# Shared rotary key in a two-layer encoder: a split-weight section of its own, or a column-tiled fp32 group on raw tokens

## The chip, the cores and the metric

One core of a Trainium2 chip. The metric is the device time of one execution in microseconds (us); a profile shows one execution, and the times are the median and the range of three.

## What is computed

Two encoder layers over 1024 tokens of width 1024, float32 throughout, then a final RMSNorm. Each layer normalises the tokens and projects them once; latent attention with 8 heads and a gated depthwise convolution of 31 taps share that projection. A gated feed-forward part follows. The part of the reference that matters here:

```
h = _rmsnorm(x, g_mix[l])
p = h @ w_in[l]
c_q = _rmsnorm(p[..., :o1], g_q[l])
...
c_kv = _rmsnorm(p[..., o1:o2], g_kv[l])
...
k_rope = _apply_rope(p[..., o2:o3], cos, sin)
...
a, gt = jnp.split(p[..., o3:], 2, axis=-1)
u = a * jax.nn.sigmoid(gt)
u = _dwconv(u, w_dw_conv[l], b_dw_conv[l])
```

`k_rope`, the shared rotary key, has 32 columns, common to all heads. `_apply_rope` needs each half of the key times cos, and the other half times sin.

## The kernel before

Features lie on partitions and tokens along the free axis: a tile is 128 features by 1024 tokens, in two halves of 512. A float32 operand is split into a rounded part (h) and a remainder (l), both fp32r, and a product takes three fp32r matmuls (high by high, high by low, low by high). The tokens are split once per layer into `hl` (xs_kh, xs_kl) with g_mix multiplied in; the row norm `rx` is applied when a product leaves PSUM.

`project` runs a layer's projections as sections on TensorE (PE). The first three, g0, a0 and g1 (gates and values of the convolution), are in `first_sections` (layer 0) and `next_sections` (layer 1). Then follow a1, g2, a2, g3, a3, kv0, kv1, kr, q0, q1, q2, k0 to k3, u0, u1 and n0 to n3, in the order of the list `seq`. Three wide PSUM slots go round: a section waits until the one three places ahead of it has been evicted by VectorE (DVE) or ScalarE (ACT). `u0` so takes the slot of `k1`, whose last reader is DVE's `kl_1` (L673).

The order on DVE is set by a planner in `project`. Each evicting routine is a generator that yields the DVE time it used and the time until its next step is due; `work(until)` runs the steps that are due, in between the convolution's near taps (`conv_step`, L1719, 1.28 us in the plan), until the DVE clock reaches the PE clock. `SECTION` holds the planned PE times of the short sections, all others count 10.9. The far taps (L1725) are multiplied on ACT and added up by accumulating transfers that GpSimd (POOL) issues. What is left of the near taps when the sections are through is placed by `work(1e9)`, ahead of attention.

The shared key is the section kr (L733 to L739). Its weight tile holds the 32 columns, rotated copy included, as 64 high and 64 low columns side by side, so that 32 fp32r matmuls of 128x512 do it. POOL casts the high part and adds up the low one, ACT negates (L180). `key_rope` (L628 to L650) then copies the lower half out of PSUM, adds it to the upper one, multiplies by rx, cos and sin, adds the two halves and splits the result for attention.

The roots of a row norm are computed by `root` and `roots`: PE turns the sums of squares (`rq0t`, L248), DVE reduces them (L259) and takes nine small steps (L263 to L271).

Of the kernel before, what the change touches and what calls it, by code (L numbers as in the profile page):

```python
# [13 lines left out]
ALU = mybir.AluOpType  # L14
# [40 lines left out]
LEAD, TURN = 33.0, 22.0  # L55
SECTION = {"kr": 7.3, "k": 2.72, "u": 4.08, "n": 4.08, "v": 2.72}
TAP = 1.28
# [59 lines left out]
class Encoder:  # L117
# [32 lines left out]
    def weight_source(self, l, name):  # L150
        a = self.a
        kind, j = name[:-1], name[-1]
        if name == "kr":
            return a["w_kr"][l]
        if name == "v":
            return a["w_v"][l]
        if name == "k":
            return a["w_k"][l].rearrange("j p c -> p j c")
        if kind == "u":
            return a["w_uq"][l, 2 * int(j):2 * int(j) + 2].rearrange("j p c -> p j c")  # L160
        return a["w_in"][l, int(j) + {"a": 0, "g": 4, "kv": 8, "q": 10}[kind]]

    def cast(self, l, name, tag="ws"):
        src = self.weight_source(l, name)
        if name != "kr":
            return self.cast_tile(src, f"w{name}{l}", tag)
        w = self.tmp(tag, f"w{name}{l}", F32R, (128, 8, 128))
        hi, lo = w[:, :, 0:64], w[:, :, 64:128]
        src = src.rearrange("p (k m) -> p k m", k=8)
        self.nc.gpsimd.dma_start(out=hi, in_=src)  # L170
        return w, hi, lo, src

# [212 lines left out]
    def first_sections(self, l, supply):  # L385
# [19 lines left out]
        def load_x(k, c=every):  # L405
            nc.sync.dma_start(out=x[k][:, c], in_=self.xd[0][k][:, c])
# [25 lines left out]
        for k in range(2, 8):  # L432
            load_x(k)
        self.ident = self.const("ident", [128, 128], self.a["ident"])
        nc.vector.tensor_copy(out=self.ones_r, in_=self.ones)
# [38 lines left out]
        for k, i in order:  # L474
# [3 lines left out]
            if (k, i) == (6, 2):  # L478
                rx = self.blk(f"rx{l}")
                for s, r in zip(HALVES, self.spread(dg, f"rx{l}", HALVES, self.bank)):  # L480
                    nc.scalar.copy(out=rx[:, s], in_=r)
        supply(-8.0)
        return hl, rx, dict(zip(names, ps))

    def next_sections(self, l, nxt, supply):
# [8 lines left out]
        for c in range(2):  # L494
            for i in range(3):
                if (c, i) == (0, 0):
                    self.upper_first(ps[i], self.tiled(w[i]), nxt["hl"], HALVES[c])
                for k in range(8 if c or i else 0):
                    self.partial(ps[i], self.tiled(w[i]), nxt["hl"], k, (c,))
                if c == 1 and i == 0:  # L500
                    self.norm_root(l, nxt, 1, self.bank)
                if c == 1 and i == 1:
                    self.norm_spread(l, nxt, 1, self.bank)
        return nxt["hl"], nxt["r"], dict(zip(names, ps))

    def upper_first(self, ps, weights, moving, c, n=8):
# [11 lines left out]
    def project(self, l, carry):  # L518
# [101 lines left out]
        def queries_norm():  # L620
# [4 lines left out]
            for t in (st["cos"], st["sin"]):  # L625
                nc.vector.tensor_tensor(out=t, in0=t, in1=r, op=ALU.mult)
                yield 1.25, 0.0

        def key_rope():
            p, cos, sin = ps["kr"], st["cos"], st["sin"]  # L630
            t = self.blk(f"krt{l}")
            nc.scalar.copy(out=t[0:64, :], in_=p[64:128, :])
            yield 0.0, 1.5
            nc.vector.tensor_tensor(out=t[0:64, :], in0=p[0:64, :], in1=t[0:64, :], op=ALU.add)
            nc.vector.tensor_tensor(out=t[0:64, :], in0=t[0:64, :], in1=rx[0:64, :], op=ALU.mult)
            nc.vector.tensor_tensor(out=t[0:32, :], in0=t[0:32, :], in1=cos[0:32, :], op=ALU.mult)
            nc.vector.scalar_tensor_tensor(out=t[32:64, :], in0=t[32:64, :], scalar=self.freq[32:64, 1:2],
                                           in1=sin[32:64, :], op0=ALU.mult, op1=ALU.mult)
            t2 = self.blk(f"krt2{l}")
            nc.scalar.copy(out=t2[0:32, :], in_=t[32:64, :])  # L640
            yield 5.0, 1.5
            nc.vector.tensor_tensor(out=t[0:32, :], in0=t[0:32, :], in1=t2[0:32, :], op=ALU.add)
# [90 lines left out]

        def shared_key():
            for k in range(8):
                for s in range(2):
                    for c in HALVES:
                        nc.tensor.matmul(ps["kr"][:, c], w["kr"][:, k, :], hl[k][s][:, c],
                                         start=(k == 0 and s == 0), stop=(k == 7 and s == 1))  # L739

        def inputs(name):
# [18 lines left out]
        def rooted(out):  # L760
# [5 lines left out]
            return st.pop(out)  # L766

        seq = []
        add = lambda name, weight, emit, evict, after=None: seq.append((name, weight, emit, evict, after))
# [9 lines left out]
        for j in range(2):  # L779
            add(f"kv{j}", f"kv{j}", inputs(f"kv{j}"), lambda j=j: latent(f"kv{j}", ckv, "kss", j))  # L780
        add("kr", "kr", shared_key, key_rope)
        add("q0", "q0", inputs("q0"), lambda: query_latent(0), lambda: root("kss", "kroot", KVL, "rkv"))
# [30 lines left out]
        launch(glu(0), -2)  # L813
        launch(gate(1), -1)
        for n, (name, weight, emit, evict, after) in enumerate(seq):
            supply(clock["pe"])
# [379 lines left out]
    def down_steps(self, l, steps, put):  # L1196
# [155 lines left out]
        def resume():  # L1352
            if not last:
                nxt["w"] = [self.cast(l + 1, n) for n in ("g0", "a0", "g1")]

        put(end - 1, 6, resume)
# [458 lines left out]
def _layout(inputs):  # L1815
# [14 lines left out]
    out["w_in"] = tiles(w_in, np.r_[o3:o3 + 2 * CONV, o1:o2, 0:o1])  # L1830
    kr = w_in[:, :, np.r_[o2:o3, o2 + HALF:o3, o2:o2 + HALF]].reshape(DEPTH, 8, 128, 64)
    out["w_kr"] = c(kr.transpose(0, 2, 1, 3)).reshape(DEPTH, 128, 512)
    hd = NOPE + ROPE
# [44 lines left out]
```

## Time and profile before

| | us |
|---|---|
| median of three runs | 2251.2 |
| range of the three | 2250.36 to 2254.52 |
| the profiled execution, its own time | 2251.68 |
| its span, first to last instruction | 2249.9 |
| PE busy in it | 2225.7 (99%) |
| DVE busy | 1687.8 (75%) |
| ACT busy | 1235.2 (55%) |
| POOL busy | 693.4 (31%) |

The profile shows one execution. Its page groups instructions by source line and tile; the timeline gives every instruction with its start and duration in us, and in brackets how long its engine was idle before it and which instruction released it. PE's rows print matmuls, PEld's their weight loads.

### The profile page before, as it was taken

How to read it: one execution, taken by the hardware profiler on the slowest of the kernel's cores; microseconds unless marked ns; L12 is line 12 of the kernel's file. 1: busy time of each engine (PE TensorE's matmuls, PEld its weight loads, DVE VectorE, ACT ScalarE, POOL GpSimd, SP SyncE). 2: the span in 40 equal slices, each digit the busy share in tenths (PEclk: the TensorE clock that was granted, in tenths of full speed). 3: DMA queues.
4: the chain of work that ended last, by engine and by line, in shares of the span. 5: the costliest groups of instructions: out<-in, count | busy, mean ns of one | idle time of the engine just before them, and what ended most of it. 6: DMA issues, size and time to landing. Idle time of an engine off the chain costs nothing. (4 is left out here: it accounts for less than half of the span.)

```text
span 2249.9 us, 34444 instructions
## 1 busy us (share of the span) xinstructions
PE 2225.7 (99%) x12746; PEld 1790.3 (80%) x12746; DVE 1687.8 (75%) x2241; ACT 1235.2 (55%) x1885; POOL 693.4 (31%) x781
## 2 busy tenths in 40 slices
PE   9999999999999999999999999999999999999998
PEld 7887666888888888888888876668888888888887
DVE  6998898669777776776559778876787777768765
ACT  5444777447655555544523457774475555555444
POOL 1221586332333332002412226652323333320032
PEclk9999999999999999999999999999999999999999
DMA  6889998765999998935968999986669999988356
GB/s 186 162 171 279 193 216 184 206 174 125 227 269 304 276 300 206 331 106 144 207 133 167 201 265 198 196 197 177 159 155 232 291 291 278 292 211 300 102 127 168
DMA packets 201160, 472.85 MB, mean 210 GB/s; under 512 B 28352, under 2 KB 35616, under 8 KB 200992
## 3 DMA queue, kind: packets, MB, share of 16 engines
q0 software_dynamic: 102704, 220.91, 48.9%
q1 hardware_dynamic: 98000, 249.35, 33.6%
q8 instruction: 100, 1.64, 0.3%
q14 instruction: 68, 0.56, 0.1%
q10 hardware_dynamic: 288, 0.39, 0.0%
HBM read 306.14 MB, written 80.40 MB: 172 GB/s over the span
## 5 line engine op out<-in xcount | busy, mean ns | idle before, releaser
L1078 PE MATMUL p<-b,w 128*128 128x512 f32 x3552 | 808.1, 389 | 0.2
L1078 PEld LDWEIGHTS p<-b,w 128*128 128x128 f32 x3552 | 665.9, 188 | 141.8 <-DVE w L1456 1.7
L1266 PE MATMUL pd<-ab,wd 128*128 128x512 f32 (+1 forms) x1920 | 422.3, 381 | 0.0
L1266 PEld LDWEIGHTS pd<-ab,wd 128*128 128x128 f32 x1920 | 350.8, 188 | 69.4 <-DVE ab L1456 0.4
L181 POOL DMA_DIRECT2D w<-wu x96 | 84.4, 879 | 358.9 <-ACT w L180 323.8
L1520 DVE TENSOR_REDUCE mx<-s 128x1 f32<-128x1024 f32 x128 | 156.2, 1220 | 37.1 <-PE s L1518 28.7
L1528 ACT ACTIVATE p<-s,mx 128x1024 f32<-128x1024 f32 x128 | 142.8, 1116 | 59.2 <-DVE mx L1520 57.3
L1468 DVE SCALAR_TENSOR_TENSOR o<-zg,par,o 128x1023 f32<-128x1023 f32 x88 | 112.8, 1283 | 76.7 <-ACT o L1462 75.3
L181 POOL DMA_DIRECT2D w<-in_w_up x116 | 100.5, 867 | 200.2 <-ACT w L180 179.0
L1719 DVE SCALAR_TENSOR_TENSOR conv<-gate,par,conv 128x1009 f32<-128x1009 f32 (+7 forms) x112 | 142.3, 1274 | 3.6 <-ACT conv L577 1.0
L180 ACT ACTIVATE w<-w 128x512 fp32r<-128x512 f32 x212 | 133.5, 630 | 3.0
L1454 ACT CAST ab<-ac 128x512 fp32r<-128x512 f32 x130 | 80.1, 617 | 97.7 <-DVE ac L1201 95.5
L1027 DVE TENSOR_TENSOR zg<-p,zg 128x512 f32<-128x512 f32 x88 | 60.5, 690 | 97.0 <-PE p L1078 90.3
L1567 PE MATMUL o<-pt,v 128*64 128x256 f32 x1024 | 126.8, 386 | 2.8 <-DVE yt L1581 1.6
L852 POOL DMA_DIRECT2D wd<-in_w_down x44 | 32.4, 738 | 308.5 <-PE pd L1266 165.2
L1468 DVE SCALAR_TENSOR_TENSOR v<-zv,par,v 128x1023 f32<-128x1023 f32 x88 | 112.4, 1279 | 10.5 <-ACT v L1462 10.4
L1454 ACT CAST w<-wu 128x512 fp32r<-128x512 f32 x84 | 51.8, 619 | 123.9 <-DVE wu L1027 121.3
L1541 PEld LDWEIGHTS t<-ident,p 64*128 64x128 f32 x2048 | 77.9, 138 | 41.1 <-issue 27.1
L1045 ACT CAST w<-wu 128x512 fp32r<-128x512 f32 x96 | 58.9, 614 | 92.9 <-DVE wu L1027 89.2
L1567 PEld LDWEIGHTS o<-pt,v 128*64 128x64 f32 x1024 | 67.9, 136 | 52.5 <-issue 18.5
L1544 DVE COPY pt<-t 128x512 f32<-128x512 f32 x128 | 87.5, 683 | 28.0 <-PE t L1541 26.8
L1738 POOL DMA_DIRECT2D conv<-late x75 | 68.3, 924 | 123.6 <-DVE late L1732 54.3
(2142 smaller groups left out, 4396.0 us busy)
## 6 DMA issues: line engine op xcount, KB each, us to landing
w<-in_w_up POOLq DMA_DIRECT2D x232, 256.0 KB, 7.4
wu<-in_w_up SPq DMA_DIRECT2D x88, 512.0 KB, 5.6
w<-wu POOLq DMA_DIRECT2D x96, 256.0 KB, 5.8
sd<-in_w_down SPq DMA_DIRECT2D x44, 512.0 KB, 9.8
ws<-sd SPq DMA_DIRECT2D x44, 512.0 KB, 6.9
wd<-in_w_down POOLq DMA_DIRECT2D x88, 256.0 KB, 5.3
act<-v SPq DMA_DIRECT2D x36, 512.0 KB, 5.7
ac<-act SPq DMA_DIRECT2D x72, 256.0 KB, 6.1
```

Of the source, the lines that this page charges most:

```text
L180: self.nc.scalar.activation(out=lo, in_=hi.bitcast(F32), func=AF.Copy, scale=-1.0)
L181: self.nc.gpsimd.dma_start(out=lo, in_=src, accum_op=ALU.add)
L1078: nc.tensor.matmul(ps, w[p][:, k * 128:(k + 1) * 128], b[:, q], start=(i in (1, 5, 2) and k == 0 and t == 0), stop=(k == 3 and t == 2), sk ...
L1266: nc.tensor.matmul(ps[t, m][:, cs], w[i, j][p][:, m * 128:(m + 1) * 128], b[:, q, cs], start=(i in (1, 5, 2) and j == 0 and s == 0), stop= ...
L1454: nc.scalar.copy(out=t[:, 0], in_=src)
L1468: self.nc.vector.scalar_tensor_tensor(out=o[:, a:b], in0=z[:, at + a:at + b], scalar=self.par[l][:, tap:tap + 1], in1=o[:, a:b], op0=ALU.m ...
L1520: nc.vector.tensor_reduce(out=mx, in_=ps, op=ALU.max, axis=AX.X, negate=True)
L1528: nc.scalar.activation(out=p, in_=ps, func=AF.Exp, bias=mx, accum_out=st["sums"][:, qt:qt + 1])
L1541: nc.tensor.transpose(t[:, i, qi, :], st["p"][2 * qp + qi][r, ks], self.ident[r, r])
L1544: nc.vector.tensor_copy(out=pt[:, :, :, 1, :], in_=tp[1])
L1567: nc.tensor.matmul(po[ROW_TILES[i % 2], cs], v[k // 2][:, k % 2, h * 64:h * 64 + 64], pt[:, i, :], start=k < 2, stop=k > 5)
L1719: self.nc.vector.scalar_tensor_tensor(out=y[:, lo:hi], in0=u[:, lo + s:hi + s], scalar=self.tap(l, j, t), in1=y[:, lo:hi], op0=ALU.mult, o ...
```

## The change

The section kr goes, and its entry in `SECTION` with it. `shared_weight` loads the 32 plain columns as one float32 tile of 128x256 (eight blocks of 32 columns) by SyncE (SP). `shared_key` multiplies it by g_mix on DVE, and then runs 16 plain fp32 matmuls of 32x512 on the raw tokens x, four groups of four: the four tiles of 32 weight columns take two blocks of rows and two token halves. It stands behind the first three sections in layer 0, and behind the first half of g1 in layer 1. Four ACT copies bring the tiles to `krt` and `krt2`; `key_sum`, launched with the first gates, adds them, multiplies by rx and makes the copy with its halves swapped by two SP transfers of 16x1024. `key_rope` runs behind kv1 and starts at the products with cos and sin. The branches for kr in `weight_source` and `cast` go.

```diff
@@ -53,7 +53,7 @@
 LEAD, TURN = 33.0, 22.0
-SECTION = {"kr": 7.3, "k": 2.72, "u": 4.08, "n": 4.08, "v": 2.72}
+SECTION = {"k": 2.72, "u": 4.08, "n": 4.08, "v": 2.72}
 TAP = 1.28
@@ -431,6 +423,7 @@
             load_x(k)
+        wk = self.shared_weight(l)
         self.ident = self.const("ident", [128, 128], self.a["ident"])
@@ -480,6 +473,7 @@
         supply(-8.0)
+        self.shared_key(l, wk, x)
         return hl, rx, dict(zip(names, ps))
@@ -497,11 +491,32 @@
                     self.partial(ps[i], self.tiled(w[i]), nxt["hl"], k, (c,))
+                if c == 0 and i == 2:
+                    self.shared_key(l, nxt["wk"], nxt["x"])
                 if c == 1 and i == 0:
...
         return nxt["hl"], nxt["r"], dict(zip(names, ps))
+
+    def shared_weight(self, l):
+        w = self.blk(f"wkr{l}", F32, (128, 8, ROPE))
+        self.nc.sync.dma_start(out=w, in_=self.a["w_kr"][l].rearrange("p (k m) -> p k m", k=8))
+        return w
+
+    def shared_key(self, l, w, x):
+        nc = self.nc
+        g = self.par[l][:, P_GMIX:P_GMIX + 8].unsqueeze(2).broadcast_to([128, 8, ROPE])
+        nc.vector.tensor_tensor(out=w, in0=w, in1=g, op=ALU.mult)
+        ps = self.bank(f"pkr{l}")
+        for i in range(4):
+            for q in range(4):
+                k = 2 * i + q % 2
+                nc.tensor.matmul(ps[q * ROPE:(q + 1) * ROPE, :], w[:, k, :], x[k][:, HALVES[q // 2]], start=i == 0, stop=i == 3,
+                                 tile_position=(0, q * ROPE))
+        self.kr = self.blk(f"krt{l}"), self.blk(f"krt2{l}")
+        for q in range(4):
+            nc.scalar.copy(out=self.kr[q % 2][0:ROPE, HALVES[q // 2]], in_=ps[q * ROPE:(q + 1) * ROPE, :])
 
@@ -626,19 +641,22 @@
 
+        def key_sum():
+            t, t2 = self.kr
+            nc.vector.tensor_tensor(out=t[0:32, :], in0=t[0:32, :], in1=t2[0:32, :], op=ALU.add)
+            nc.vector.tensor_tensor(out=t[0:32, :], in0=t[0:32, :], in1=rx[0:32, :], op=ALU.mult)
+            for i in range(2):
+                nc.sync.dma_start(out=t[32 + i * HALF:48 + i * HALF, :], in_=t[HALF - i * HALF:ROPE - i * HALF, :])
+            yield 2.5, 0.0
+
         def key_rope():
-            p, cos, sin = ps["kr"], st["cos"], st["sin"]
-            t = self.blk(f"krt{l}")
-            nc.scalar.copy(out=t[0:64, :], in_=p[64:128, :])
-            yield 0.0, 1.5
-            nc.vector.tensor_tensor(out=t[0:64, :], in0=p[0:64, :], in1=t[0:64, :], op=ALU.add)
-            nc.vector.tensor_tensor(out=t[0:64, :], in0=t[0:64, :], in1=rx[0:64, :], op=ALU.mult)
+            t, cos, sin = self.kr[0], st["cos"], st["sin"]
             nc.vector.tensor_tensor(out=t[0:32, :], in0=t[0:32, :], in1=cos[0:32, :], op=ALU.mult)
...
                                            in1=sin[32:64, :], op0=ALU.mult, op1=ALU.mult)
-            t2 = self.blk(f"krt2{l}")
+            t2 = self.blk(f"krt3{l}")
             nc.scalar.copy(out=t2[0:32, :], in_=t[32:64, :])
-            yield 5.0, 1.5
+            yield 2.5, 1.5
             nc.vector.tensor_tensor(out=t[0:32, :], in0=t[0:32, :], in1=t2[0:32, :], op=ALU.add)
@@ -731,13 +749,6 @@
 
-        def shared_key():
-            for k in range(8):
-                for s in range(2):
-                    for c in HALVES:
-                        nc.tensor.matmul(ps["kr"][:, c], w["kr"][:, k, :], hl[k][s][:, c],
-                                         start=(k == 0 and s == 0), stop=(k == 7 and s == 1))
-
         def inputs(name):
@@ -765,6 +776,11 @@
 
+        def shared_latent(j):
+            yield from latent(f"kv{j}", ckv, "kss", j)
+            if j:
+                yield from key_rope()
+
         seq = []
@@ -777,8 +793,7 @@
         for j in range(2):
-            add(f"kv{j}", f"kv{j}", inputs(f"kv{j}"), lambda j=j: latent(f"kv{j}", ckv, "kss", j))
-        add("kr", "kr", shared_key, key_rope)
+            add(f"kv{j}", f"kv{j}", inputs(f"kv{j}"), lambda j=j: shared_latent(j))
         add("q0", "q0", inputs("q0"), lambda: query_latent(0), lambda: root("kss", "kroot", KVL, "rkv"))
@@ -812,6 +827,7 @@
         launch(gate(1), -1)
+        launch(key_sum(), 0)
         for n, (name, weight, emit, evict, after) in enumerate(seq):
@@ -1352,6 +1368,7 @@
                 nxt["w"] = [self.cast(l + 1, n) for n in ("g0", "a0", "g1")]
+                nxt["wk"] = self.shared_weight(l + 1)
 
@@ -1828,8 +1845,8 @@
     out["w_in"] = tiles(w_in, np.r_[o3:o3 + 2 * CONV, o1:o2, 0:o1])
-    kr = w_in[:, :, np.r_[o2:o3, o2 + HALF:o3, o2:o2 + HALF]].reshape(DEPTH, 8, 128, 64)
-    out["w_kr"] = c(kr.transpose(0, 2, 1, 3)).reshape(DEPTH, 128, 512)
+    kr = w_in[:, :, o2:o3].reshape(DEPTH, 8, 128, ROPE)
+    out["w_kr"] = c(kr.transpose(0, 2, 1, 3)).reshape(DEPTH, 128, 8 * ROPE)
     hd = NOPE + ROPE
```

The plan moves instructions beyond the diff. Three places on DVE, word for word as the programs have them; `conv_3` is the convolution's fourth block of channels, `128x1018` the length of a near tap. In layer 0 between q1's squares (`qss_1`) and the remainder of the second normalised latent (`kvs_1l`), before:

```order
L607 TENSOR_TENSOR qss_1127<-qss_1127,qss_1_1232 128x1024
L660 SCALAR_TENSOR_TENSOR kvs_0l<-ckv_918,par_63,kvs_0h 128x1024
L616 TENSOR_TENSOR ckv_968<-ckv_968,rkv_1153 128x1024
L1719 SCALAR_TENSOR_TENSOR conv_3_845<-gate_3_777,par_63,conv_3_845 128x1018
L660 SCALAR_TENSOR_TENSOR kvs_1l<-ckv_968,par_63,kvs_1h 128x1024
```

and in the changed program:

```order
L622 TENSOR_TENSOR qss_1110<-qss_1110,qss_1_1215 128x1024
L678 SCALAR_TENSOR_TENSOR kvs_0l<-ckv_950,par_63,kvs_0h 128x1024
L631 TENSOR_TENSOR ckv_1022<-ckv_1022,rkv_1136 128x1024
L1736 SCALAR_TENSOR_TENSOR conv_3_878<-gate_3_809,par_63,conv_3_878 128x1012
L1736 SCALAR_TENSOR_TENSOR conv_3_878<-gate_3_809,par_63,conv_3_878 128x1013
L678 SCALAR_TENSOR_TENSOR kvs_1l<-ckv_1022,par_63,kvs_1h 128x1024
```

One tap stood ahead of `kvs_1l`, now two, and they are earlier taps. In layer 0 around the remainder of the second key section (`kl_1`) and the root for the queries (`rq0t`), before:

```order
L660 SCALAR_TENSOR_TENSOR cqs_2l<-cq_1269,par_63,cqs_2h 128x1024
L1719 SCALAR_TENSOR_TENSOR conv_3_845<-gate_3_777,par_63,conv_3_845 128x1020
L673 TENSOR_TENSOR kl_1_1328<-pk_1273,kh_1_1327 128x1024
L259 TENSOR_REDUCE rq0t<-rq0t 128x4 x2
L263 TENSOR_SCALAR rq0v<-rq0t 128x8
L264 TENSOR_SCALAR rq0y<-rq0v 128x8
```

and in the changed program:

```order
L251 TENSOR_REDUCE rq0t<-rq0t 128x4 x2
L255 TENSOR_SCALAR rq0v<-rq0t 128x8
L256 TENSOR_SCALAR rq0y<-rq0v 128x8
L257 TENSOR_TENSOR rq0t<-rq0y 128x8
L258 TENSOR_TENSOR rq0t<-rq0t,rq0v 128x8
L259 SCALAR_TENSOR_TENSOR rq0t<-rq0t 128x8
L260 SCALAR_TENSOR_TENSOR rq0y<-rq0t,rq0y 128x8
L261 TENSOR_TENSOR rq0t<-rq0y 128x8
L262 SCALAR_TENSOR_TENSOR rq0t<-rq0t,rq0v 128x8
L263 SCALAR_TENSOR_TENSOR rq0y<-rq0t,rq0y 128x8
L691 TENSOR_TENSOR kl_1_1312<-pk_1257,kh_1_1311 128x1024
L691 TENSOR_TENSOR kl_2_1338<-pk_1298,kh_2_1337 128x1024
```

`kl_1` stood ahead of the reduction; now it stands behind the reduction and its nine small steps. In layer 1 it is the same, and there three taps stand between q1's squares and `kl_1` that stood earlier before. In layer 0 at the end of the projections, where DVE turns to attention (`v_0` a copy of the values, `mx_0_0` the first row maximum), before:

```order
L721 SCALAR_TENSOR_TENSOR qn_1_1551<-qn_1_1551,qns_1_1553 128x1024
L721 SCALAR_TENSOR_TENSOR qn_2_1574<-qn_2_1574,qns_2_1576 128x1024
L721 SCALAR_TENSOR_TENSOR qn_3_1578<-qn_3_1578,qns_3_1580 128x1024
L1506 COPY v_0_1609<-pv_1_1611 128x512
L1520 TENSOR_REDUCE mx_0_0_1640<-s_0_0_1629 128x1
```

and in the changed program:

```order
L739 SCALAR_TENSOR_TENSOR qn_3_1562<-qn_3_1562,qns_3_1564 128x1024
L1736 SCALAR_TENSOR_TENSOR conv_3_878<-gate_3_809,par_63,conv_3_878 128x1018
L1736 SCALAR_TENSOR_TENSOR conv_3_878<-gate_3_809,par_63,conv_3_878 128x1019
L1736 SCALAR_TENSOR_TENSOR conv_3_878<-gate_3_809,par_63,conv_3_878 128x1020
L1736 SCALAR_TENSOR_TENSOR conv_3_878<-gate_3_809,par_63,conv_3_878 128x1021
L1736 SCALAR_TENSOR_TENSOR conv_3_878<-gate_3_809,par_63,conv_3_878 128x1022
L1523 COPY v_0_1598<-pv_1_1600 128x512
L1537 TENSOR_REDUCE mx_0_0_1629<-s_0_0_1618 128x1
```

Five taps now stand between the last query remainder and the first copy. In layer 1 no tap stands there, before or now. On SP the two transfers of the key's copy stand ahead of the load of the positions in layer 0, and ahead of the loads of cos and sin in layer 1.

## Rows read from the trace of the kernel before

**Rows 1.** Page: busy time by engine; shares of the chain of waits.

```profile
PE 2225.7 (99%) x12746; PEld 1790.3 (80%) x12746; DVE 1687.8 (75%) x2241; ACT 1235.2 (55%) x1885; POOL 693.4 (31%) x781
...
PE 39%; DVE 2%; issue 1%; DMA 1%; ACT 0%; POOL 0%; DVEq 0%; POOLq 0%; SPq 0%; ACTq 0%
```

**Rows 2.** Timeline of PE, layer 0's shared key: start us, duration us, operation.

```profile
118.95 0.62 PE L738 MATMUL pkr<-xs_0h,wkr 128*128 128x512 f32 x2
...
126.21 0.62 PE L217 MATMUL pq<-xs_0h,wq00h 128*128 128x512 f32 x2
```

**Rows 3.** Windows, shared key alone: length; busy PE, PEld, DVE, ACT; clock; DMA.

```profile
0.00:2249.00 2249.00, 14.83 (x64) 12.01 (x64) 2.42 (x2) 2.03 (x2) 1.00 0.83 210
```

**Rows 4.** Timeline of PE at the start: plain fp32, then fp32r.

```profile
1.06 5.06 PE L399 MATMUL warm<-ones 128*128 128x128 f32 x22 [1.06 <-DVE ones L374]
5.77 0.98 PE L470 MATMUL pg<-xs_0h,wg00h 128*128 128x512 f32 x2
6.59 0.97 PE L470 MATMUL pg<-xs_0l,wg00h 128*128 128x512 f32 x2
```

**Rows 5.** Timeline of PE in attention: plain fp32, two 64-column tiles.

```profile
219.36 1.95 PE L1567 MATMUL o<-pt,v 128*64 128x256 f32 x16
221.24 0.72 PE L1541 MATMUL t<-ident,p 64*128 64x64 f32 x16
```

**Rows 6.** Source view, L1567: its weight loads, ns min/median/max.

```profile
L1567 PEld LDWEIGHTS o<-pt,v x1024: 132/137/137, 219.4 to 1517.2; 128*64 128x64 f32 x171
```

**Rows 7.** Timeline of ACT, layer 0, q2; idle before and releaser in brackets.

```profile
149.52 1.07 ACT L613 COPY rkv<-rkv0s 128x512 f32<-128x512 f32 x2 [4.34 <-PE rkv0s L286]
...
155.00 1.15 ACT L1725 ACTIVATE far<-gate,par 128x1020 f32<-128x1020 f32 x1 [1.36 <-DMA conv<-far]
```

**Rows 8.** Timeline of DVE, layer 0, from q1's squares on.

```profile
157.12 1.23 DVE L607 TENSOR_TENSOR qss<-qss,qss 128x1024 f32<-128x1024 f32 x1 [3.36 <-ACT qss L605]
...
160.60 1.27 DVE L1719 SCALAR_TENSOR_TENSOR conv<-gate,par,conv 128x1018 f32<-128x1018 f32 x1
...
171.32 1.22 DVE L673 TENSOR_TENSOR kl<-pk,kh 128x1024 fp32r<-128x1024 f32 x1
172.45 1.28 DVE L259 TENSOR_REDUCE rq0t<-rq0t 128x4 f32<-128x512 f32 x2
...
175.46 1.22 DVE L673 TENSOR_TENSOR kl<-pk,kh 128x1024 fp32r<-128x1024 f32 x1
```

**Rows 9.** Timeline of PE, layer 0: k3 and u0 start.

```profile
170.08 0.71 PE L217 MATMUL pk<-kvs_0h,wk0h 128*128 128x512 f32 x2
...
172.89 0.62 PE L217 MATMUL pu<-cqs_0h,wu20h 128*128 128x512 f32 x2
```

**Rows 10.** Timeline of DVE, layer 0, end of the projections.

```profile
203.02 0.68 DVE L1506 COPY v<-pv 128x512 f32<-128x512 f32 x1
205.34 1.23 DVE L1520 TENSOR_REDUCE mx<-s 128x1 f32<-128x1024 f32 x1 [1.64 <-PE s L1518]
```

**Rows 11.** Timeline of ACT, same stretch: the first exponential.

```profile
206.60 1.12 ACT L1528 ACTIVATE p<-s,mx 128x1024 f32<-128x1024 f32 x1 [0.76 <-DVE mx L1520]
```

**Rows 12.** Timeline of PE, same stretch: the third score tile starts.

```profile
211.10 0.49 PE L1518 MATMUL s<-kn,qns 64*128 64x512 f32 x1
```

**Rows 13.** Timeline of ACT, layer 1, around q2.

```profile
1267.78 1.15 ACT L1725 ACTIVATE far<-gate,par 128x1020 f32<-128x1020 f32 x1 [1.99 <-DMA conv<-far]
```

**Rows 14.** Timeline of DVE, layer 1, from q1's squares on.

```profile
1269.91 1.22 DVE L607 TENSOR_TENSOR qss<-qss,qss 128x1024 f32<-128x1024 f32 x1 [5.67 <-ACT qss L605]
...
1278.27 1.23 DVE L607 TENSOR_TENSOR qss<-qss,qss 128x1024 f32<-128x1024 f32 x1 [1.13 <-ACT qss L605]
...
1283.00 1.28 DVE L259 TENSOR_REDUCE rq1t<-rq1t 128x4 f32<-128x512 f32 x2
```

**Rows 15.** Timeline of PE, layer 1: u0 starts.

```profile
1285.73 0.62 PE L217 MATMUL pu<-cqs_0h,wu21h 128*128 128x512 f32 x2
```

**Rows 16.** Timeline of DVE, layer 1, around the new group's place.

```profile
1143.88 0.16 DVE L263 TENSOR_SCALAR rx_512v<-rx_512p 128x4 f32<-128x4 f32 x1 [13.56 <-PE rx_512p L238]
```

More of the change, by code (lines that the diff above doesn't have):

```diff
@@ L152, in weight_source @@
         kind, j = name[:-1], name[-1]
-        if name == "kr":
-            return a["w_kr"][l]
         if name == "v":
@@ L164, in cast @@
         src = self.weight_source(l, name)
[L165 to L171, printed above, removed]
+        return self.cast_tile(src, f"w{name}{l}", tag)
     def cast_tile(self, src, name, tag="ws"):
```

## The prediction

> **What bounds the kernel now.** I read the page first. TensorE is busy for 2225.7 of the 2249.9 us span, and the chain that ended last gives VectorE 2% and transfers 1% beside it [rows 1]. So a change pays only if it shortens PE's own work, and costs if it makes PE wait. Then I read the timelines at the places where the order of the changed kernel differs: the shared-key section, the stretch from q1's squares to u0, and the turn to attention. The profiled execution took 2251.68 us (span 2249.9), 0.5 above the median of 2251.2. The sum below is made against 2251.68; the forecast is then moved down by 0.5. A measurement here can tell 0.2%, which is 4.5 us, from no change.
>
> **PE's own work.** Removed: in layer 0 the 32 matmuls of the shared key run from 118.95 to the first of q0 at 126.21, 7.26 us, with q0 directly behind [rows 2]. The windows row counts 64 for both layers, 14.83 busy [rows 3], so layer 1 loses as much.
>
> Added, per layer: 16 plain fp32 matmuls of 32x512 on four tiles. No row shows four column tiles. A plain fp32 matmul makes two records: the 11 warming ones print as 22. They go at (5.77 - 1.06) / 22 = 0.214 us per 128 columns, where fp32r beside them takes (6.59 - 5.77) / 2 = 0.41 per 512, or 0.103 per 128 [rows 4]. So a plain record costs 2.1 times an fp32r record of the same width. In attention eight plain matmuls, 16 records of 256 columns, on two 64-column tiles, take 221.24 - 219.36 = 1.88 us, 0.1175 each [rows 5]. An fp32r record of 256 columns costs 7.26 / 64 = 0.113, so twice its price is what one tile would need alone: the two tiles run side by side. One tile alone then needs 0.235 per 256 columns. The new group has 32 records of 512: 15.0 us one at a time, 7.5 two at a time, 3.76 four at a time. I take 3.76, since in the nearest row no tile slows the other; the ends for the range are 3.76 and 7.5, with 15.0 beyond. **Per layer PE gains 7.26 - 3.76 = 3.5 us** from q0 on.
>
> Two tiles together draw their moving data at the pace of one fp32r matmul; four would draw double, which no row shows. That is the first rival. On the weight loads a row and a rule differ: the 16 loads of the attention group, 0.137 each [rows 6], sum to 2.19, more than the 1.88 that loads and matmuls take together, so most are hidden. The Trainium skill ("TensorE: Matmul & The Clock Gate", section "Part 3: Packing small matmuls — row/col tiling") says that weight loads overlap running matmuls only where the row groups differ; here all four tiles use all rows, as both tiles of the attention group do, and the trace speaks against it. Without hiding, 32 loads x 0.137 = 4.4 us would come on top, 8.1 for the group.
>
> **Layer 0, the wait at u0.** u0 takes the PSUM slot of k1, so it waits until DVE has done kl_1. DVE's chain to there starts with q1's squares at 157.12, behind ACT [rows 8]. ACT was idle for 4.34 us for PE's rkv0s and once more for 1.36 us for a far tap's transfer [rows 7]. So the chain hangs on PE and moves up with it by 3.5. It ends with kl_1 at 171.32 + 1.22 = 172.54, 15.42 after its start [rows 8]; u0 started at 172.89 [rows 9], 0.35 later. In the changed order two things stand ahead of kl_1 that did not: one tap more, 1.27, and the reduction with the nine root steps, 175.46 - 172.45 = 3.01 [rows 8]. The chain becomes 15.42 + 1.27 + 3.01 = 19.70 and kl_1 ends at 157.12 - 3.5 + 19.70 = 173.32, less what the far tap's wait gives back, 0 to 1.36. I take half, 0.7: 172.6. PE could be at u0 at 172.89 - 3.5 = 169.39. It waits some 3.2, and **only 0.3 of the 3.5 is left**.
>
> There is a floor. The reduction follows PE's turned sums, which end about where k3 starts; k3 lasts 172.89 - 170.08 = 2.81 [rows 9], while reduction, roots and kl_1 need 3.01 + 1.22 = 4.23. So 1.4 per layer is lost at u0 even if DVE is never late.
>
> **Layer 0, the turn to attention.** The planner has 7.3 us less per layer to place taps, and five now stand ahead of the first copy of v. From DVE's 203.02 - 0.3: five taps 6.35, the copy 0.68, the maximum 1.23 [rows 10], and the exponential with its sum some 1.2 [rows 11], which gives 212.2. The third score tile takes the first one's slot and started at 211.10 [rows 12]. So **layer 0 ends 1.1 later than before**: DVE, not PE, is late there.
>
> **Layer 1.** Same wait, other numbers. From 1269.91 to 1283.00, where kl_1 ends and the reduction starts, are 13.09, with 1.13 idle in it [rows 14]. Three taps that were done earlier now fall in it: 13.09 - 1.13 + 3.81 + 3.01 = 18.78. From 1269.91 - 3.5 this gives 1285.19, less 0 to 1.99 from ACT's wait for a far tap [rows 13]; with half, 1284.2, against u0's 1285.73 [rows 15]. **Layer 1 gains 1.5.** At its end no tap moves ahead of attention.
>
> **Edits that cost nothing on the path.** The product of w_kr with g_mix, 128x256, falls in layer 1 into 13.56 us of DVE's idle time [rows 16], and in layer 0 behind the first roots, ahead of the group. Four short ACT copies delay the first sigmoid; section a1 with 10.9 us of the plan covers it. If that cover were gone the second glu would be late and a slot with it, by about 2 us. The key's sum (two DVE operations of 32 partitions) takes the place of two of 64. SP now issues the two small transfers ahead of the positions (layer 0) and of cos and sin (layer 1), and waits at them for the key's sum; the positions are used some sections later. POOL loses the cast and the accumulating transfer of w_kr; nothing waited for them.
>
> **Sum.** +1.1 - 1.5 = -0.4 on 2251.68: 2251.3, and against the median about 2250.8; I say 2251.0. With the two far-tap ends the forecast's own range is 2249 to 2253.
>
> **Rivals.**
> *Feed limit, slower.* If four tiles can draw no more moving data than the two of the attention group, the group takes 7.5 us. Every chain above hangs on PE, so each us over 3.76 costs two: 2251.0 + 2 x 3.74 = 2258.5. It decides from about 6.1 us, where 2 x 2.35 = 4.7 is over the band. For it: two tiles already match the fp32r pace exactly. Against: neither tile was slowed. 0.10.
> *Weight loads exposed, slower.* 8.1 us, 2251.0 + 2 x 4.4 = 2259.8. Rows 6 speak against it. 0.03.
> *No tiles side by side.* 15.0 us: 2251.0 + 2 x 11.2 = 2273. The attention group speaks against it. 0.03.
> *The waits are at their floor, faster.* If the far taps never hold ACT and DVE is early, u0 waits only 1.4. Layer 0: -3.5 + 1.4 at u0 and 1.4 more at the third score tile (212.5 against 211.10, both moved up), -0.7; layer 1: -2.1. That is -2.8, 2248.4 against the median. If in addition the three taps or the five lie in idle time, the 1.4 goes too, and with a group at its shortest about -5.5: 2245.7. For it: ACT idles 4.34 before its copies. Against: 3.81 and 6.35 us of taps have nowhere else to go in the written order. 0.25, about half of it below 2246.7.
>
> **How the numbers follow.** My forecast, the freed time given back at u0 and at the turn to attention, has 0.59. Range: 2245.5 to 2255.0 takes in the forecast and all of the floor case, and a group of up to 5.7 us; it leaves out the slower rivals, 0.16, and a little more. Faster by over 0.2%: 0.13; slower: 0.10 + 0.03 + 0.03 = 0.16; within: 0.71.
>
> **What would show it.** In the changed profile the new group spans 3.7 to 4.7 us from its first to the next section's first matmul; 7 or more means the feed limit. PE idles about 3 us at u0 in both layers, released by kl_1, and DVE's chain from q1's squares to kl_1 takes near 19 us. In layer 0 the third score tile waits for ACT's exponential by 1 to 2 us behind five taps. If PE runs into u0 with less than 1.5 us of idle time, the forecast is wrong on the faster side; if PE idles ahead of gate or glu sections, the edits that I cost at nothing were not.

## The result, and the profile after

The changed kernel takes 2256.55 us (median of 12 runs, 2253.31 to 2259.94), the kernel before 2251.03 in the runs beside it: 1.0023 times as long, with a 95% interval of 1.0015 to 1.003. It is 5.5 us slower. The forecast was 2251.0 with a range up to 2255.0. The profiled execution has a span of 2255.8 us, 5.9 more than the 2249.9 before.

The page of the changed kernel, busy time by engine and the shares of the chain that ended last [rows 1]:

```profile
PE 2221.7 (98%) x12746; PEld 1781.7 (79%) x12746; DVE 1689.8 (75%) x2243; ACT 1236.2 (55%) x1888; POOL 694.3 (31%) x778
...
PE 84%; DVE 6%; issue 5%; DMA 3%; POOL 1%; ACT 1%; SPq 0%; DVEq 0%; POOLq 0%; ACTq 0%
```

PE works 4.0 us less than before, and the span is 5.9 longer. So PE idles some 10 us more. The new group itself is as short as forecast; the timeline of PE in layer 0, start and duration in us, the next section in the second row:

```profile
43.51 3.64 PE L515 MATMUL pkr<-x,wkr 128*32 128x512 f32 x32
47.08 0.73 PE L209 MATMUL pa<-xs_0h,wa10h 128*128 128x512 f32 x2
```

From 43.51 to 47.08 are 3.57 us, against 7.26 for the old section [rows 2]: 32 records on four tiles, faster than the 3.76 worked out from the two tiles of attention [rows 5].

To see where the rest went, the same matmul of both profiles is compared: the change's start less the start before.

| PE starts | after less before, us | step |
|---|---|---|
| layer 0, a1 | +4.29 | group 3.7; 0.6 lies in the first loads |
| q0 | -2.84 | old section gone |
| u0 | -0.57 | waits 2.3 longer |
| first value-times-weights product of attention | +1.03 | turn to attention, 1.6 |
| layer 1, a0 | +4.47 | layer 0's attention 3.8, of which 0.3 is given back behind it |
| a1 | +8.26 | group 3.8 |
| q0 | +1.01 | old section gone |
| u0 | +3.59 | waits 2.6 longer |
| the spread of the queries' root | +5.31 | low clock, 1.7 |
| first value product | +6.81 | waits for a PSUM slot, 1.5 |
| last operation | +5.82 | layer 1's attention, -1.0 |

**u0 in layer 0.** The timeline of DVE, and that of PE (in brackets the idle time before; "issue" here is a wait that the profile puts down to no instruction):

```profile
167.99 1.28 DVE L251 TENSOR_REDUCE rq0t<-rq0t 128x4 f32<-128x512 f32 x2
...
171.00 2.35 DVE L691 TENSOR_TENSOR kl<-pk,kh 128x1024 fp32r<-128x1024 f32 x2
```

```profile
172.32 0.70 PE L209 MATMUL pu<-cqs_0h,wu20h 128*128 128x512 f32 x2 [2.55 <-issue]
```

The reduction and the nine root steps stand ahead of kl_1, as the order said; the row at 171.00 holds kl_1 and kl_2, 1.2 each, so kl_1 ends at 172.2 and u0 starts at 172.32 [rows 8, 9]. The chain to there starts with q1's squares:

```profile
152.62 1.23 DVE L622 TENSOR_TENSOR qss<-qss,qss 128x1024 f32<-128x1024 f32 x1 [2.39 <-ACT qss L620]
```

**The turn to attention in layer 0**, DVE and then PE:

```profile
202.56 6.54 DVE L1736 SCALAR_TENSOR_TENSOR conv<-gate,par,conv 128x1018 f32<-128x1018 f32 x5
209.03 0.68 DVE L1523 COPY v<-pv 128x512 f32<-128x512 f32 x1
209.63 1.21 DVE L1537 TENSOR_REDUCE mx<-s 128x1 f32<-128x1024 f32 x1
```

```profile
209.76 0.50 PE L1519 MATMUL pv<-wv0h,kvs_0h 128*128 128x512 f32 x1 [1.80 <-DVE v L1523]
...
212.13 0.50 PE L1535 MATMUL s<-kn,qns 64*128 64x512 f32 x1 [0.70 <-ACT p L1545]
```

Five taps take 6.54 us. A value product waits 1.80 for DVE's copy, and the third score tile starts at 212.13 for the exponential, 1.03 later than at 211.10 before [rows 10 to 12].

**Layer 0's attention** is new. DVE, POOL and PE around the first place where it falls back:

```profile
244.43 2.22 DVE L1749 TENSOR_SCALAR late<-gate,par 128x1021 f32<-128x1021 f32 x1
246.57 0.27 DVE L1618 COPY rs<-sr 8x128 f32<-8x128 f32 x1
246.77 0.67 DVE L1561 COPY pt<-t 128x512 f32<-128x512 f32 x1
```

```profile
243.75 2.36 POOL L1753 TENSOR_TENSOR conv<-conv,late 128x1018 f32<-128x1018 f32 x1
```

```profile
247.50 0.65 PE L1558 MATMUL t<-ident,p 64*128 64x64 f32 x14 [0.56 <-DVE pt L1561]
```

A late tap on DVE, a product with one factor, takes 2.22 us here, where others take 0.74. It starts while POOL adds two tiles, and it ends 0.54 after POOL does. The copy of the turned probabilities behind it comes late, and PE waits. POOL's own late taps do the same; DVE, then POOL:

```profile
362.36 1.95 DVE L1749 TENSOR_SCALAR late<-gate,par 128x1010 f32<-128x1010 f32 x1
```

```profile
362.36 1.42 POOL L1749 TENSOR_SCALAR late<-gate,par 128x1009 f32<-128x1009 f32 x1
```

Eleven late taps of DVE begin in layer 0's attention while POOL is at an operation. Nine of them end 0.54 to 0.56 after POOL's operation, whether they take 0.85 us or 2.90: their end hangs on POOL's and not on their own start. The other two took 0.74. The Trainium skill ("SBUF — State Buffer", section "Summary: rules for kernel authors") says: "If DVE is in 2-port perf mode, or has two SBUF inputs while the GpSimd op reads SBUF, the second one to issue **fully blocks** until the first finishes." The trace agrees as to the blocking, with these nine of eleven; in which mode DVE ran no trace here shows. What the meetings cost is in the groups by line for DVE, 200 to 430 us, first of the kernel before, then of the changed one (count, busy us, mean ns):

```profile
L1732 DVE TENSOR_SCALAR late<-gate,par 128x1019 f32<-128x1019 f32 (+14 forms) x25 | 24.4, 975 | 0.1
```

```profile
L1749 DVE TENSOR_SCALAR late<-gate,par 128x1020 f32<-128x1020 f32 (+14 forms) x25 | 28.5, 1140 | 0.1
```

25 late taps took 24.4 us before and 28.5 now. The 4.1 us more are near the 3.8 by which layer 0's attention grew. In layer 1 it is the other way, 27.2 before and 24.6 now, and its attention shrank by 1.0. As many taps run on DVE as before; what changed is when each falls against POOL's work. In layer 0 eight taps met POOL before and eleven do now, but before, six of the eight met one of POOL's own taps (1.4 us alone), and now eight of the eleven meet an operation on two tiles, such as the addition (2.4 us alone).

**Layer 1 at u0**, DVE, then PE, and two windows (length; PE, PEld and DVE busy with counts, and so on; then PE's clock, DMA share, GB/s):

```profile
1288.00 3.48 DVE L691 TENSOR_TENSOR kl<-pk,kh 128x1024 fp32r<-128x1024 f32 x3
```

```profile
1289.32 0.70 PE L209 MATMUL pu<-cqs_0h,wu21h 128*128 128x512 f32 x2 [2.39 <-issue]
...
1290.58 1.05 PE L209 MATMUL pu<-cqs_0l,wu21h 128*128 128x512 f32 x2
```

```profile
1289.30:1293.70 4.40, 4.38 (x12) 3.50 (x13) 2.18 (x2) 0.00 (x0) 0.00 (x0) 0.61 1.03 282
1293.70:1300.00 6.30, 6.30 (x33) 5.25 (x32) 3.13 (x3) 1.09 (x2) 0.00 (x0) 1.00 1.03 418
```

DVE's chain to kl_1 starts here with the squares at 1270.70:

```profile
1270.70 1.23 DVE L622 TENSOR_TENSOR qss<-qss,qss 128x1024 f32<-128x1024 f32 x1 [4.20 <-ACT qss L620]
```

kl_1 ends at 1289.2 and PE has idled 2.39. Then two matmuls take 0.85 between starts instead of 0.45: the granted clock is 0.61 on average over the next 4.4 us, which is its lower level, 1.2 GHz, for 3.4 us of them. Before, u0 started without a wait [rows 15].

**The first value product of layer 1** waits for the eviction of the last section; before (first row) it did not wait:

```profile
1311.11 0.39 PE L1502 MATMUL pv<-wv1h,kvs_0h 128*128 128x512 f32 x1
...
1317.92 0.50 PE L1519 MATMUL pv<-wv1h,kvs_0h 128*128 128x512 f32 x1 [1.32 <-DVE qn L731]
```

**What was costed at nothing and cost nothing.** ACT's copies and a table load behind them push the first sigmoid back, and DVE with it (ACT, then DVE):

```profile
47.22 2.37 ACT L519 COPY krt<-pkr 32x512 f32<-32x512 f32 x4 [4.35 <-PE pkr L515]
49.60 1.28 ACT L583 ACT_TABLE_LOAD   x1
50.90 1.06 ACT L583 ACTIVATE gate<-gate 128x1024 f32<-128x1024 f32 x1
```

```profile
51.99 1.23 DVE L585 TENSOR_TENSOR gate<-gate,rx 128x1024 f32<-128x1024 f32 x1 [9.80 <-ACT gate L583]
```

DVE idles 9.80 us ahead of that gate, and it starts 7.3 later than the same row before did. PE still keeps the distance of +4.42 from g2 to kv1, without a wait: section a1 and DVE's slack covered it.

### The profile page after: what moved, and what is told of

Same layout as the page of the kernel before. It is cut to its first block, busy times and chain, and to the rows that moved or that the text cites. A ratio compares the mean times of both kernels' runs of the same rounds, so it can differ in the third digit from the quotient of the medians.

```text
span 2255.8 us, 34453 instructions
## 1 busy us (share of the span) xinstructions
PE 2221.7 (98%) x12746; PEld 1781.7 (79%) x12746; DVE 1689.8 (75%) x2243; ACT 1236.2 (55%) x1888; POOL 694.3 (31%) x778
## 4 chain that ended last, share of the span: by engine, by line
PE 84%; DVE 6%; issue 5%; DMA 3%; POOL 1%; ACT 1%; SPq 0%; DVEq 0%; POOLq 0%; ACTq 0%
PE p L1094 33%; PE pd L1282 19%; PE po L905 7%; PE s L1535 5%; PE o L1584 4%; PE t L1558 3%; PE pg L530 2%; PE pa L209 1%; PE pq L209 1%; PE pn L209 1%; DVE mx L1537 1%; PE pkv L209 1%; PE pg L209 1%; PE pa L530 1%; DMA w<-wu 1%
## 5 line engine op out<-in xcount | busy, mean ns | idle before, releaser
L1584 PEld LDWEIGHTS o<-pt,v 128*64 128x64 f32 x1024 | 67.9, 136 | 51.9 <-issue 18.5
```

What stands on the lines that cost most here:

```text
L1584: nc.tensor.matmul(po[ROW_TILES[i % 2], cs], v[k // 2][:, k % 2, h * 64:h * 64 + 64], pt[:, i, :], start=k < 2, stop=k > 5)
```

## The experiments

Theory A: the group is worth its 3.7 us a layer, and the order that the planner makes without the 7.3 us takes it back and more. The rival B: what the change adds (copies, transfers) costs. The ratios compare each run with the kernel before on the same chip, whose medians there were 2252.1 to 2252.7. The changed kernel's 2256.55 stood beside 2251.03, so a difference from it is uncertain by 1 to 2 us.

**The old kernel with the new plan.** Nothing of the shared key changes; only its planned time goes to zero.

```diff
-SECTION = {"kr": 7.3, "k": 2.72, "u": 4.08, "n": 4.08, "v": 2.72}
+SECTION = {"kr": 0.0, "k": 2.72, "u": 4.08, "n": 4.08, "v": 2.72}
```

> The kernel before, with its shared-key section on TensorE as it was, but planned at 0 us instead of 7.3, so that VectorE's order is nearly that of the changed kernel (roots ahead of kl_1 in both layers, five taps ahead of attention in layer 0, as many far taps). Theory A (the order of the work costs, the new group does not): the waits of the changed kernel come back without its 7 us of gain: 2.3 at u0 and 1.5 at attention's start in layer 0, some 3 in layer 0's attention, 2.6 + 1.7 at u0 and 1.5 before attention in layer 1, so 2259 to 2265 us. Theory B (what the change adds costs: ScalarE's copies ahead of the first sigmoid, the transfers of the key's copy ahead of the positions): the old kernel keeps its time, 2250 to 2253 us.

Measured: 2263.62 us, 1.0055 times the kernel before (1.004 to 1.007). The timeline of PE at u0 in both layers:

```profile
175.39 1.19 PE L217 MATMUL pu<-cqs_0h,wu20h 128*128 128x512 f32 x2 [2.48 <-issue]
...
1294.90 1.19 PE L217 MATMUL pu<-cqs_0h,wu21h 128*128 128x512 f32 x2 [2.55 <-issue]
```

The waits are those of the changed kernel, with the low clock behind u0 in both layers, and the third score tile is 5.5 late. Layer 0's attention grew by only 0.9 here (0.7 up to layer 1's a0), so that term is not part of the order as such but of the moment. None of the added operations is in this kernel, and it loses 11 us: B is not needed for the loss. That the added operations cost nothing is not shown by this run, but by the mended runs below, which have them and keep the group's gain.

**kl_1 ahead of the roots** in the changed kernel:

```diff
-            pending[out] = [clock["pe"] + 2.0, steps(), 99]
+            pending[out] = [clock["pe"] + (3.0 if key == "qss" else 2.0), steps(), 99]
```

> The changed kernel with the queries' root due 1 us later in the plan, so that VectorE does kl_1 ahead of the reduction and the nine root steps; two of the five last taps also move earlier. Theory A (u0 waits for kl_1 alone, and the low clock in layer 1 follows that wait): TensorE idles under 0.5 us ahead of u0 in both layers instead of 2.55 and 2.39, no stretch at the low clock in layer 1 (1.7 us), together some 6 us faster than the changed kernel: 2249 to 2252 us. Theory B (VectorE's total work sets when attention starts): u0 starts earlier, but the time is lost again ahead of attention in each layer, 2255 to 2257 us.

Measured: 2249.35 us, 0.9989 (0.998 to 0.9999): 7.2 faster than the changed kernel by the medians (its ratio was 1.0023), and a little faster than the one before. PE, layer 0 and layer 1:

```profile
168.79 0.62 PE L209 MATMUL pk<-kvs_1l,wk0h 128*128 128x512 f32 x2
169.24 0.61 PE L209 MATMUL pu<-cqs_0h,wu20h 128*128 128x512 f32 x2
...
1282.55 0.62 PE L209 MATMUL pk<-kvs_1l,wk1h 128*128 128x512 f32 x2
1283.01 0.62 PE L209 MATMUL pu<-cqs_0h,wu21h 128*128 128x512 f32 x2
```

u0 follows k3 without a gap in both layers, and no stretch behind it is slow. Two of the five last taps moved too, and the turn to attention costs 0.4 instead of 1.6. Layer 0's attention still grows, by 4.0, and the value product of layer 1 still waits 1.32: these two do not hang on u0.

**No late tap on DVE**, in the changed kernel and in the one before:

```diff
-LATE_VECTOR = (2, 3)
+LATE_VECTOR = ()
```

> The changed kernel with no late tap on VectorE during attention (GpSimd does them all; the same taps in the same total). Theory A (layer 0's attention grew by 3.4 us because late taps on VectorE now meet GpSimd's additions and take 2 us instead of 0.74): layer 0's attention, from its first o product to the last transposes, shrinks by 3 us or more, and the kernel takes 2250 to 2254 us, unless GpSimd then ends late. Theory B (attention grew because it starts later or because of transfers): its length stays, 2255 to 2258 us.

> The kernel before with the same edit, as the control for the run ahead of it. Theory A: it gains less than the changed kernel, since fewer of its late taps met GpSimd's additions: the distance between the two (5.5 us) shrinks to 2 to 3 us; 2247 to 2251 us. Theory B: both move alike and the distance stays near 5.5 us.

Measured: 2259.86 (1.0033, 1.002 to 1.0046) for the changed kernel, 2245.80 (0.9975, 0.9966 to 0.9985) for the one before. As times both missed, and the distance, expected at 2 to 5.5, grew to 14 us. The trace shows why: layer 0's attention of the changed kernel no longer grows (+3.85 late when attention begins, +3.57 at layer 1's a0), where it grew by 3.4, and layer 1's gains 4.6 up to 1455 us. Then comes one new wait, of PE, behind ACT, behind POOL:

```profile
1499.65 1.97 PE L1584 MATMUL o<-pt,v 128*64 128x256 f32 x8 [6.75 <-ACT pt L1560]
```

```profile
1498.49 0.63 ACT L172 ACTIVATE wo<-wo 128x512 fp32r<-128x512 f32 x1 [8.91 <-DMA wo<-in_w_o]
1499.03 0.57 ACT L1560 COPY pt<-t 128x512 f32<-128x512 f32 x1
```

POOL in the changed kernel, then in the one before, both with this edit:

```profile
1490.12 2.49 POOL L868 DMA_DIRECT2D wo<-in_w_o  x4
```

```profile
1476.53 2.49 POOL L852 DMA_DIRECT2D wo<-in_w_o  x4
```

POOL, now with all late taps, issues the loads of the output weights at 1490.12. ACT stands at them for 8.91 us, the copy that PE needs is queued behind, PE idles 6.75, and the clock is at its lower level for 6.8 us from 1497.69 on, within that wait and behind it: some 9 us together. The kernel before has one late tap less in layer 1 (48 against 49); with the same edit it issues those loads at 1476.53 and PE does not wait. Of the 13.6 us between the two issues, 7.9 is the later start of attention; that the rest is the tap more was not tried. The profile of the changed kernel, the slowest of its five executions, also has 3.4 us at the lower level in the first loads and as much at u0 of each layer.

Taking the taps away shows that the growth needs them. How it goes with their lengthening can be read from all five profiles of a changed order that leave 25 late taps per layer on DVE (attention from its first o product to its last turn; two of the runs follow below). In layer 0 the two rise together, in layer 1 more loosely:

| against the kernel before, us | layer 0: late taps, attention | layer 1: late taps, attention |
|---|---|---|
| changed kernel | +4.1, +3.8 | -2.6, -1.0 |
| old kernel, new plan | +1.1, +0.9 | +1.7, 0.0 |
| kl_1 ahead of the roots | +5.2, +4.2 | +0.7, +0.9 |
| wait at u0 filled | +2.6, +2.3 | +3.1, +1.0 |
| another PSUM slot | +5.0, +3.4 | -4.2, -2.9 |

**The wait at u0 filled** with matmuls whose product nobody reads:

```diff
+        def held_clock():
+            fill = self.bank(f"fill{l}")
+            for i in range(9):
+                nc.tensor.matmul(fill, hl[0][0][:, 0:128], hl[0][0][:, 0:512], start=True, stop=True)
+
...
             finish(n - 3)
+            if name == "u0":
+                held_clock()
             ps[name] = self.wide(f"p{name}{l}")
```

> The changed kernel with nine matmuls of 128x512 whose product nobody reads, ahead of u0 in both layers: they fill TensorE's wait for kl_1. Theory A (the wait brings the low clock, which then costs a time of its own): no stretch at the low clock behind u0 of layer 1, whose matmuls go back from 0.43 to 0.23 us; u0 to the queries' spread matmuls takes 4.1 us as before and not 5.8; 1.5 to 2 us faster than the changed kernel, 2254 to 2256 us. Theory B (those matmuls are slow for another reason, such as traffic): the stretch stays slow, 2256 to 2258 us.

```profile
1285.84 2.20 PE L787 MATMUL fill<-xs_0h 128*128 128x512 f32 x9
1288.30 0.73 PE L209 MATMUL pu<-cqs_0h,wu21h 128*128 128x512 f32 x2 [0.26 <-DVE kl L691]
...
1292.52 1.03 PE L278 MATMUL rq1s<-ident,rq1y 128*128 128x128 f32 x8
```

Measured: 2256.84 us (1.0024, 1.0012 to 1.0036), no gain, so the time missed. In the profile the section runs at full clock: 4.22 us from u0 to the spread matmuls, 5.80 in the changed kernel. But the low clock came elsewhere, for 3.4 us at the waits of layer 0's turn to attention, and the mean granted clock over its six executions, 0.998, is that of the changed kernel's twelve. Nor does one such profile show that the fill did it, since the wait alone does not always bring the low clock. This is u0 of layer 1 in the changed kernel with fewer late taps on DVE (the last group of runs):

```profile
1286.65 0.70 PE L209 MATMUL pu<-cqs_0h,wu21h 128*128 128x512 f32 x2 [2.37 <-issue]
...
1290.85 0.82 PE L278 MATMUL rq1s<-ident,rq1y 128*128 128x128 f32 x6
```

The wait is there, and the section takes 4.20. Over all profiles it comes out so: of ten places at u0 where PE waited 2.34 to 2.58 us, six have 3.4 us at the lower level; of sixteen where it waited under 0.5, none. So the low clock at u0 goes with the wait, but does not come each time.

**Another PSUM slot**, no instruction moved:

```diff
-        self.pp.tile([128, T], F32, name=f"skip{l}", tag="w1", bufs=1)
+        self.pp.tile([128, T], F32, name=f"skip{l}", tag="w2", bufs=1)
```

> The changed kernel with the unused PSUM tile that shifts layer 1's addresses put on w2 instead of w1; no instruction moves. Theory A (with one section fewer the first value product of layer 1's attention falls on the slot of the last section and waits for its eviction): the 1.3 us wait ahead of the first value product in layer 1 goes, 1 to 1.5 us faster than the changed kernel, 2254.5 to 2256 us. Theory B (VectorE is late there whatever the slot): the wait moves to the third value product or the first score tile, same time as the changed kernel within 0.5 us.

Measured: 2254.39 us (1.0013, 1.000 to 1.0025). PE at the first value product of layer 1:

```profile
1314.66 0.62 PE L209 MATMUL pn<-cqs_2l,wu11h 128*128 128x512 f32 x2
1315.11 0.39 PE L1519 MATMUL pv<-wv1h,kvs_0h 128*128 128x512 f32 x1
```

No wait is left there, and none came in its place up to the third score tile. By the medians the gain is 2.2 us, which its interval does not tell from the expected 1 to 1.5. The kernel before had 24 sections going round three slots, now there are 23, so the last section fell on the slot that attention takes first.

**Three mends together**: the roots, the slot, and late taps on DVE for the fourth block alone (`LATE_VECTOR = (3,)`) or for none.

> The changed kernel with three mends together: kl_1 ahead of the roots, the unused tile on w2, and late taps on VectorE for the convolution's fourth block alone (the third block's go to GpSimd). Theory A (the costs are separate and add up): 2249.4 of the run with kl_1 first, less 1.3 for the slot, less about 2 to 4 for half of the meetings of VectorE and GpSimd: 2243 to 2247 us. Theory B (what one mend frees another wait takes): 2248 to 2251 us.

> The same with no late tap on VectorE. Theory A: layer 0's attention gains 4 us and layer 1's 4 to 5 against the run with kl_1 first, 2239 to 2243 us, if GpSimd issues the loads of the output weights in time at the end of layer 1's attention. Theory B (GpSimd with one more late tap in layer 1 than the kernel before issues them too late): a wait of 5 us or more there and the low clock behind it, as in the run with the changed kernel, 2247 to 2253 us.

Measured: 2241.26 us (0.9962, 0.9947 to 0.9977) for the first, 2250.17 (0.9997, 0.9988 to 1.0007) for the second. The second has the wait for the output weights again, 5.69 us of PE, and 6.8 us of the low clock. The page of the first:

```profile
PE 2217.2 (99%) x12746; PEld 1778.9 (79%) x12746; DVE 1667.6 (74%) x2224; ACT 1235.8 (55%) x1888; POOL 713.3 (32%) x797
```

PE works 8.5 us less than before. It is at u0 3.9 earlier than before in layer 0 and 7.4 in layer 1, and ends 11.4 earlier; the last 4 come from layer 1's attention.

**The controls**: the old kernel and the changed kernel with `LATE_VECTOR = (3,)` alone, and the mended one again.

> The kernel before with late taps on VectorE for the fourth block alone: the control for the run with three mends (the kernel before has kl_1 ahead of the roots, and its value product on a free slot, anyway). Theory A (the new group is worth its 3.6 to 3.7 us per layer wherever the order does not take them): 2246 to 2249 us, 6 to 8 us above the run with three mends. Theory B (the run with three mends is fast through the late taps alone): 2240 to 2243 us, the same.

> The changed kernel with that edit alone: kl_1 behind the roots and the slot as in the changed kernel. Theory A: 2241.3 of the run with three mends plus what the two waits cost, 2.5 and 2.4 at u0 with up to 1.7 for a low clock, 1.3 at the value product: 2247 to 2250 us, which is no better than the old kernel with the same edit. Theory B (the late taps are all that matters): 2241 to 2244 us.

> The run with three mends once more, for its interval beside its control: 2240 to 2243 us by either theory.

Measured: 2250.64 (0.9992, 0.9983 to 1.0001), 2252.32 (1.0001, 0.999 to 1.0011), and 2243.07 (0.9962, 0.9948 to 0.9977). The old kernel and the changed one gain less from the edit than expected: each stands about 2 us above its range. The changed kernel is 9.3 us above the mended one on the same chip, where its expectation added up 6.2 to 7.9. The distance between old and mended is 7.6 us, where two groups are worth 2 x 3.7 = 7.4: with the same late taps, the mended change keeps its gain. That the two figures are so near is in part luck: in the profiles the two groups bring 3.8 and 3.5, and the attentions of the two layers differ by some 2 and -1. Nor is this the old kernel's best setting. With no late tap on DVE it took 2245.80, a ratio of 0.9975 against 0.9962 for the mended one, which is 2.9 us, and the intervals overlap.

## Why the prediction was wrong

- **PE's own work**, 3.5 a layer: right, 3.7. The feed limit and exposed weight loads fall with 3.57 us for the group.
- **u0 in layer 0**, 0.3 left of 3.5: right. DVE's chain from q1's squares took 19.6 us, forecast 19.70; u0 ended up 0.57 ahead. The 0.6 lost in the first loads did not show at u0, since DVE and not PE sets its start; PE waited 2.55 instead of 3.2.
- **The turn to attention**, 1.1 late: right, 1.03, by the copy and the exponential behind five taps.
- **u0 in layer 1**, a gain of 1.5 for the layer: the chain was right (18.5 us, forecast 18.78), what ACT's wait for a far tap gives back was not: 1.0 was taken, 0.2 came. The gain was 0.9.
- **The step that failed is the sum**: it ended at u0 and at the first scores, and held without a reason that nothing behind them would move. Three terms stood at nothing. The largest is attention itself: layer 0's cost 3.4 more up to layer 1's a0, with as many operations in it, since DVE's late taps now met POOL's longer operations; layer 1's gave back 1.0. The wait at u0 was priced as its length, but in the profiled execution's layer 1 it brought the low clock, 1.7 us. "At its end no tap moves ahead of attention" was true, and yet the first value product of layer 1 came 1.5 late, since a section less shifts which slot is taken. Together 5.6 us, and with the 0.6 at u0 of layer 1 it is 6.2, the distance from the sum's -0.4 to the +5.8 of the profiled execution. By the medians the distance is 5.5. One profile of each kernel stands behind the single terms; how much the low clock takes differs from execution to execution.
- Of the rivals none described this. The slower ones all put the loss into the group. The floor case, a wait of 1.4 at u0, did not occur; kl_1 ahead of the roots gave a time near it, 2249.35, by taking away what the floor was made of.

Not settled: how much of the 5.5 us each run pays for meetings of DVE and POOL, since that depends on the moment (4.1 us of lengthening in one profile of layer 0, with nearly the same order 1.1 in another, and in layer 1 less than before); and why the same wait at u0 brings the low clock at one time and not at another. Taking away POOL's side of the meetings was not tried; the runs took the DVE side away.

## What to carry to other kernels

Where a planner's table sets the order, taking a section out of the table is a change of its own: run the old kernel with the new table, and the price of the order stands by itself (here 11 us, against 7.4 that the faster work is worth). Behind the last wait that a sum looks at, check three things: which slots the rotation now hands to whom, whether the added idle time of TensorE is followed by a low clock, and whether two engines that shut each other out meet more often, or at longer operations. A root that nobody needs yet should not stand ahead of an eviction that TensorE waits for: moving it one step, with two taps that moved along, gave 7 us.

## What the runs showed of the hardware

Four 32-column tiles of plain fp32 ran side by side: 32 records of 512 columns in 3.57 us, 0.112 each, where an fp32r record of that width takes 0.227. So four tiles went through twice the columns of a full-width fp32r matmul in the same time, and no slower than the two-tile group of attention foretells (3.76). A DVE product with one factor, 0.74 us alone, that began while POOL was at an operation took up to 2.90 us; in layer 0's attention nine of eleven ended 0.54 to 0.56 after POOL's operation, seven of eight in the kernel before, whether that read one tile or two. Behind or within an idle time of PE of 2.34 to 2.58 us at u0 the clock stood at its lower level for 3.4 us at six of ten places, and at the other four it did not: in the changed kernel behind 2.39 us in layer 1 and not behind 2.55 in layer 0, in the old kernel with the new plan and with no late tap on DVE in both layers, with another PSUM slot in layer 0 alone, and with fewer late taps on DVE in neither.
